# SwiGLU gate and up products: a pair's second block takes S2 before S1, blocks 1 to 10 begin S2's PSUM bank with the kept sum, and bank copies get a higher priority

## The chip, the cores and the metric

The kernel runs on one core of one Trainium2 chip. The metric is the device time of one execution in microseconds (us), lower is better. The core's engines each work through a queue of their own: PE (TensorE, matmuls, with PEld for its weight loads), DVE (VectorE), ACT (ScalarE), POOL (GpSimd, used here mostly to issue DMAs) and SP (SyncE, which issues DMAs). Matmuls write into PSUM, which has eight banks; a bank holds one 128 x 512 result in float32.

## The reference

One encoder block: a token mixer, then a SwiGLU feed-forward layer, each between two RMS norms. The change lies in the feed-forward layer's first product.

```
def swiglu(h, w_gate_up, w_down):
    gu = jnp.einsum("bsd,df->bsf", h, w_gate_up)
    g, u = jnp.split(gu, 2, axis=-1)
    return jnp.einsum("bsf,fd->bsd", jax.nn.silu(g) * u, w_down)
...
for l in range(DEPTH):
    h = rmsnorm(x, norm_mix_pre[l])
    m = mixer(h, w_in[l], b_f[l], conv_w[l], w_branch[l], w_out[l])
    x = x + rmsnorm(m, norm_mix_post[l])
    h = rmsnorm(x, norm_ffn_pre[l])
    f = swiglu(h, w_gate_up[l], w_down[l])
    x = x + rmsnorm(f, norm_ffn_post[l])
```

There are 1024 tokens, 1024 model columns and 2816 hidden columns, all in float32.

## The kernel before

**Products.** A float32 product is made from three matmuls on operands split into a high and a low part (`mm3`). ACT writes the high part (`hi`, a copy), DVE the low part (`lo`, source minus high). `prod` runs four blocks of 128 along the contraction, so a product on a 128 x 512 bank is 12 matmuls. Large products go by a Winograd form of Strassen's scheme: seven products A11, A12, A22, S1 to S4 of sums of weight blocks, each with its partner of the activations (B11, B21, B22, T1 to T4), whose results are summed to the four quarters.

**The gate and up product.** Hidden columns come in 22 blocks of 128 (`f` = 0 to 21); a block's gate and up weights and the two halves of the tokens are the four quarters. A block's weights are loaded by SP (`raw` tiles, 512 KB each), summed on DVE (`sx`, and in place in `raw`) and split. Three kinds of operand pairs come out of it: one for A11 and A12 (`prep_first`), one for S2 and S3 (from `sx`), one for S1 and A22 (from the second `raw`) (`prep_rest`). Their tiles come from one pool: three `raw`, four `hi`, three `lo`, one `sx`. A tile can be written again when the last product that reads it is done.

**Blocks 0 to 10** had A11 and A12 done in an earlier stage (`f_begin`, `f_end`). Two sums of each are kept: `p1` (A11's product) and `g1` (the gate quarter). For blocks 0 and 1 they stay in the tile `um`, for the others they go through DRAM (`pre_dram`) and come back by loads that POOL issues, into two tiles for `p1` and two for `g1`. Class `Rest` (from line 2098) does what is left: S2 into bank `b2`; DVE adds `p1` to it, giving `c12`; ACT copies `c12` back into the bank; S1 goes into `b3`; S3 is accumulated on `b2`; ACT copies the bank to `c22`, DVE adds `b3`; A22 is accumulated on `b2`, S4 on `b3`; ACT takes the Silu of `g1` and DVE multiplies it with `b2`. The loop at line 2129 interleaves two blocks, so that PE's order is S3(f), S2(f+1), A22(f), S4(f), S1(f+1), S3(f+1).

**Block 11** goes alone (`strassen`). **Blocks 12 to 21** go in five pairs x, y (`two_blocks`, line 2052): each has six products of its own, and their S4 products are done together by a second level of the scheme, seven half-width products (`prod2`, six matmuls of 256 columns each) into bank `zb` and the halves of `b3`. The loop fixes PE's order:

```
for step in (x.a11, x.s1, x.s2, x.a12, x.s3):
    step()
more()
for step in (y.a11, x.a22, y.s1, y.s2, y.a12, y.s3):
    step()
```

after which come the half-width products, with y.a22 before the last of them. `more()` prepares the next pair's x block (`prep_even`). In a block, A11, S2, S3 and A22 are accumulated one upon the other in bank `b1`, and after each ACT copies the bank out (`c11`, `c12`, `c22`) before the next is added; the tiles for these are halves of `um`.

**Order on the engines.** PE's order in the pair stage is the program's (`strict`). The order on ACT, DVE, POOL and SP is made when the kernel is built, by a planner that gives each engine, among the instructions that it holds to be ready, the one with the best priority; priority is the place in the program, and `ahead(call, by)` (line 125) moves it `by` places to the front. On the chip each engine then works in that fixed order.

**Afterwards** come the down product (bank names `pd`) and the last norm, with PE busy to the end.

Of the kernel before, what the change touches and what calls it, by code (L numbers as in the profile page):

```python
# [36 lines left out]
VF = AW + H  # L37
HV = VF // 2
TAIL = 4
NPRE = 11  # L40


B11, B21, B22, T1, T2, T3, T4 = range(7)
A11, A12, A22, S2, S3, S4, S1 = range(7)
# [3 lines left out]
def block_kernel(  # L48
# [16 lines left out]
    n1, n2 = slice(0, NC), slice(NC, S)  # L65
# [44 lines left out]
    def add(o, a, b):  # L110
        nc.vector.tensor_tensor(o, a, b, op=ALU.add)
# [13 lines left out]
    def ahead(call, by=80):  # L125
        with tc.high_priority(offset=by):
            call()

    def copy(o, a):
        nc.scalar.activation(o, a, AF.Copy)  # L130

    def split(hi, lo, src):

        copy(hi, src)
        sub(lo, src, f32(hi))

    def mm3(ps, a, b, start, stop, **kw):

        ah, al = a
        bh, bl = b  # L140
        nc.tensor.matmul(ps, ah, bh, start=start, stop=False, **kw)
        nc.tensor.matmul(ps, ah, bl, start=False, stop=False, **kw)
        nc.tensor.matmul(ps, al, bh, start=False, stop=stop, **kw)
# [14 lines left out]
    }  # L158
    pre_dram = [dpool.tile([2, P, NC], F32, name=f"pre_dram{f}") for f in range(NPRE)]
    ri_dram = [dpool.tile([2, S], F32, name=f"ri_dram{j}") for j in range(4)]  # L160
# [383 lines left out]
    def raw_t():  # L544
        return wtile("raw", 3)

    def hi_t():
        return wtile("hi", 4, F32R)

    def lo_t():  # L550
        return wtile("lo", 3, F32R)
# [10 lines left out]
    def kmaj(src):  # L562
        return src.rearrange("(k p) m -> p k m", p=P)
# [3 lines left out]
    def prep_first(src1, there=None):  # L567

        if there is None:
            r1 = raw_t()  # L570
            nc.sync.dma_start(r1, kmaj(src1))
            h1, l1 = hi_t(), lo_t()
            split(h1, l1, r1)
        else:
            r1, h1, l1 = there
        return dict(A11=(h1[:, LO], l1[:, LO]), A12=(h1[:, UP], l1[:, UP])), r1

    def prep_rest(src2, r1, behind=False, keep=None):

        r2 = raw_t()  # L580
        nc.sync.dma_start(r2, kmaj(src2))
        a11, a12, a21, a22 = r1[:, LO], r1[:, UP], r2[:, LO], r2[:, UP]
        sx = wtile("sx", 1)
        s2, s3 = sx[:, LO], sx[:, UP]
        (pinned if behind else lambda call, _: call())(lambda: sub(s3, a11, a21), "vector")
        s1 = a21
        add(s1, a21, a22)
        sub(s2, s1, a11)
        hx, lx = hi_t(), lo_t()
        split(hx, lx, sx)  # L590
        h2, l2 = hi_t(), lo_t()
        split(h2, l2, r2)
        ops = dict(
            S2=(hx[:, LO], lx[:, LO]), S3=(hx[:, UP], lx[:, UP]),
            S1=(h2[:, LO], l2[:, LO]), A22=(h2[:, UP], l2[:, UP]),
        )
        s4 = a12 if keep == "there" else s4_t()
        sub(s4, a12, s2)
        if keep:
            return {**ops, "S4": s4, "raw": r1}  # L600
        h4, l4 = s4h_t(), s4l_t()
        split(h4, l4, s4)
        return {**ops, "S4": (h4, l4)}
# [13 lines left out]
    def prod(ps, w, b, first):  # L617
        (ah, al), (bh, bl) = w, b
        kw = {} if first else dict(skip_group_check=True)
        for k in range(4):  # L620
            mm3(
                ps,
                (ah[:, k, :], al[:, k, :]),
                (bh[:, k, :], bl[:, k, :]),
                first and k == 0,
                k == 3,
                **kw,
            )
# [63 lines left out]
    def wcols(c0):  # L692
        return win[:, c0 : c0 + P]
# [352 lines left out]
    for ij, (kind, j, _, _) in enumerate(jobs):  # L1046
# [12 lines left out]
        if ij < 2:  # L1059
            if ij == 0:  # L1060
                r1 = raw_t()
# [13 lines left out]
            w = {**w, **prep_rest(wcols(jobs[ij][3]), r1)}  # L1075
# [3 lines left out]
        elif ij < len(jobs) - 1:  # L1079
# [3 lines left out]
            w = pairs.get()  # L1083
# [3 lines left out]
        else:  # L1087
            w = pairs.get()
# [14 lines left out]
        elif kind == "gb":  # L1103
            for m, parts in ((j, (c11, c12)), (j + 1, (c21, c22))):
                zt = zts.pop(m)
                for n in range(2):
                    o = n * NC
# [340 lines left out]
    def both(t):  # L1448
        return t[:, 0], t[:, 1]
# [320 lines left out]

    FIRSTS = [*range(2, NPRE), 0, 1]
    begun, kept = {}, {}
# [21 lines left out]
    hb = [both(h2b11)]  # L1794
# [84 lines left out]

    for n in range(4, NPRE + 1):  # L1880
        if n < NPRE:
            f_begin(n, bank(psm, "b1"), first_tile(n, "c21", 7))
# [4 lines left out]
        if n == 8:  # L1887
            for sl in range(4):
                a = slice(sl * P, (sl + 1) * P)
                b = slice(NC + sl * P, NC + (sl + 1) * P)  # L1890
# [29 lines left out]
    def gated(f, ns, g, u, t=None):  # L1920
        y = y_slot(f)[:, ns]
        t = y if t is None else t
        nc.scalar.activation(t, g, AF.Silu)
        mul(y, t, u)
# [14 lines left out]
    left, right = slice(0, NC // 2), slice(NC // 2, NC)  # L1939
# [62 lines left out]

    def prep_even(f):
        a, b = f_src(f)
        w, r1 = prep_first(a)
        return {**w, **prep_rest(b, r1, keep="own")}

    def prep_odd(f, even):
# [5 lines left out]
    class Block:  # L2014
# [5 lines left out]
        def a11(self):  # L2020
            self.b1, self.c11 = bank(psm, "b1"), t_(later, "c21")
            prod(self.b1, self.w["A11"], hb[B11], True)
            copy(self.c11, self.b1)

        def s1(self):
            self.b3 = bank(psm, "b3")
# [2 lines left out]
        def s2(self):  # L2029
            self.c12 = t_(later, "c12")  # L2030
            prod(self.b1, self.w["S2"], hb[T2], False)
            copy(self.c12, self.b1)

        def a12(self):
            b2 = bank(psm, "b2")
            prod(b2, self.w["A12"], hb[B21], True)
            add(self.c11, self.c11, b2)

        def s3(self):
            self.c22 = t_(later, "c22")  # L2040
            prod(self.b1, self.w["S3"], hb[T3], False)
            copy(self.c22, self.b1)
            add(self.c22, self.c22, self.b3)

        def a22(self):
            prod(self.b1, self.w["A22"], hb[T4], False)
            gated(self.f, n1, self.c11, self.b1)

        def end(self):
            gated(self.f, n2, self.c12, self.c22)  # L2050
# [1 line left out]
    def two_blocks(x, y, w2, more):  # L2052

        tq = um[:, 7, n1]
        for step in (x.a11, x.s1, x.s2, x.a12, x.s3):
            step()
        more()
        for step in (y.a11, x.a22, y.s1, y.s2, y.a12, y.s3):
            step()
        zb_ = bank(psm, "zb")  # L2060
        prod2(zb_[:, right], w2["S1"], hb2[T1], True)
        prod2(zb_[:, left], w2["A11"], hb2[B11])
        copy(tq[:, left], zb_[:, left])
        prod2(x.b3[:, left], w2["A12"], hb2[B21])
        prod2(x.b3[:, right], w2["S4"], hb2[B22])
        add(x.c12, x.c12, x.b3)
        prod2(y.b3[:, left], w2["A22"], hb2[T4])
        add(y.c12, y.c12, y.b3)
        prod2(zb_[:, left], w2["S2"], hb2[T2])
        copy(tq[:, right], zb_[:, left])  # L2070
        y.a22()
        prod2(zb_[:, left], w2["S3"], hb2[T3])

        def ends():
            add(x.c12, x.c12, tq)
            for b in (x, y):
                add(b.c12[:, right], b.c12[:, right], zb_[:, right])
            for n in (left, right):
                add(y.c12[:, n], y.c12[:, n], zb_[:, left])
            x.end()  # L2080
            y.end()

        return ends
# [9 lines left out]

    rest = Pairs([f_src(f) for f in range(NPRE)], prep_rest_alone)
    for _ in range(2):
        rest.more()

    class Rest:


        def __init__(self, f):
            self.f, self.w = f, rest.get(False)
            if f in kept:
                self.p1, self.g1 = kept[f]
            else:
                self.p1 = t_(fp, "c21")
                nc.gpsimd.dma_start(self.p1, pre_dram[f][0])
                self.g1 = z_tile("c11", w=NC)
                nc.gpsimd.dma_start(self.g1, pre_dram[f][1])
            self.b2, self.c12 = bank(psm, "b2"), t_(fp, "c12")  # L2110
            prod(self.b2, self.w["S2"], hb[T2], True)
            add(self.c12, self.p1, self.b2)
            copy(self.b2, self.c12)

        def two(self):
            self.b3, self.c22 = bank(psm, "b3"), t_(fp, "c22")
            prod(self.b3, self.w["S1"], hb[T1], True)
            prod(self.b2, self.w["S3"], hb[T3], False)
            copy(self.c22, self.b2)
            add(self.c22, self.c22, self.b3)  # L2120

        def end(self):
            prod(self.b2, self.w["A22"], hb[T4], False)
            prod(self.b3, self.w["S4"], hb[B22], False)
            gated(self.f, n1, self.g1, self.b2, self.g1)
            add(self.c12, self.c12, self.b3)
            gated(self.f, n2, self.c12, self.c22, self.c12)

    now = Rest(0)
    for f in range(NPRE):  # L2130
        now.two()
# [17 lines left out]
    for f in range(NPRE + 1, NF, 2):  # L2149
# [4 lines left out]
        x, y = Block(f, even), Block(f + 1, odd)  # L2154
# [275 lines left out]
```

## Time and profile before

| what | value |
|---|---|
| median of 3 runs | 1320.42 us (1319.51 to 1320.93) |
| the profiled execution's own time | 1319.99 us |
| its span in the trace | 1318.2 us |
| mean granted TensorE clock | 0.998 of full speed |
| stage of blocks 0 to 11, in the trace | about 737 to 907 us |
| five pairs, in the trace | about 907 to 1101 us |
| down product and the end | 1101 us to the end |

The profile shows one execution: busy time by engine, the waits with what ended them, the chain of work that ended last, and the instructions in order of time. A name such as `lo<-raw,hi` is "output <- inputs" by tile names; `b` stands for the banks `b1`, `b2` and `b3`, `c` for tiles such as `c12`, `c22`, `c21`. All instructions show line 77, the helper that issues them, so the tile names tell them apart. A matmul's row spans 0.39 us, but the next one starts about 0.227 us after it.

### The profile page before, as it was taken

The numbers are of one execution on the slowest core, as the hardware profiler recorded it, in microseconds if no ns is written. First come the engines' busy times: TensorE is split into PE (matmuls) and PEld (weight loads), VectorE is DVE, ScalarE is ACT, GpSimd is POOL, SyncE is SP. The second block draws the span as 40 slices with busy tenths as digits, with TensorE's granted clock in tenths as the row PEclk, the third lists the DMA queues.
The fourth block names the chain that finished last, engine by engine and source line by source line (L and its number), as shares of the span: only waits on it lengthen the run. The fifth ranks groups of instructions, "written<-read, shape, count | busy, mean of one in ns | idle before, by whom it ended". The sixth has DMA issues, their size and how long they took to land.

```text
span 1318.2 us, 18276 instructions
## 1 busy us (share of the span) xinstructions
PE 1302.3 (99%) x6776; PEld 1087.7 (83%) x6776; DVE 966.5 (73%) x1509; ACT 608.4 (46%) x977; POOL 154.9 (12%) x289
## 2 busy tenths in 40 slices
PE   9999999999999999999999999999999999999997
PEld 9988888888888888888878888888888788888886
DVE  6975979875656877587797677777676667676685
ACT  6642433253355866445677434333343334444452
POOL 0001100011112212020012012211100110000000
PEclk9999999999999999999999999999999999999999
DMA  6347757768646544499376456543322338866441
GB/s 219 112 119 224 196 161 208 191 211 232 176 144 200 162 140 157 148 346 367 114 242 207 134 162 194 188 130 102 120 78 99 104 120 292 304 249 195 157 167 65
DMA packets 207242, 235.15 MB, mean 178 GB/s; under 512 B 12064, under 2 KB 150368, under 8 KB 207152
## 3 DMA queue, kind: packets, MB, share of 16 engines
q1 hardware_dynamic: 159136, 156.08, 37.7%
q0 software_dynamic: 18832, 63.22, 13.1%
q10 hardware_dynamic: 29184, 14.68, 4.5%
q8 instruction: 53, 0.87, 0.3%
q14 instruction: 37, 0.30, 0.1%
HBM read 161.79 MB, written 72.16 MB: 177 GB/s over the span
## 4 chain that ended last, share of the span: by engine, by line
PE 91%; DVE 3%; ACT 2%; DMA 2%; issue 1%; DVEq 0%; POOL 0%; ACTq 0%; POOLq 0%
PE b L77 52%; PE pd L77 16%; PE pba L77 3%; PE pv L77 3%; PE tps L77 3%; PE po L77 3%; PE sp L77 2%; PE p L77 2%; PE pbp L77 2%; PE pbv L77 1%; PE zb L77 1%; DMA raw<-in_w_gate_up_dram 1%; DVE lo L77 1%; PE ma L77 1%; PE q L77 1%
## 5 line engine op out<-in xcount | busy, mean ns | idle before, releaser
L77 PE MATMUL b<-x,hi 128*128 128x512 f32 x1088 | 335.8, 390 | 0.7 <-ACT b L77 0.7
L77 PEld LDWEIGHTS b<-x,hi 128*128 128x128 f32 x1088 | 203.4, 188 | 43.1 <-ACT b L77 1.1
L77 PE MATMUL b<-x,lo 128*128 128x512 f32 x544 | 212.6, 391 | 4.3 <-DVE lo L77 4.3
L77 DVE TENSOR_TENSOR lo<-raw,hi 128x1024 fp32r<-128x1024 f32 x90 | 108.4, 1204 | 89.7 <-PE b L77 71.0
L77 ACT ACTIVATE hi<-raw 128x1024 fp32r<-128x1024 f32 (+1 forms) x96 | 97.4, 1017 | 80.5 <-PE b L77 43.0
L77 PEld LDWEIGHTS b<-x,lo 128*128 128x128 f32 x544 | 102.1, 188 | 27.8 <-DVE lo L77 6.8
L77 DVE TENSOR_TENSOR c<-c,b 128x512 f32<-128x512 f32 x120 | 81.7, 682 | 30.8 <-PE b L77 22.6
L77 ACT ACTIVATE hi<-sx 128x1024 fp32r<-128x1024 f32 (+1 forms) x42 | 43.8, 1042 | 80.9 <-PE b L77 71.6
L77 DVE TENSOR_TENSOR sx<-raw 128x512 f32<-128x512 f32 x78 | 53.6, 688 | 24.4 <-DMA raw<-in_w_gate_up_dram 12.6
L77 DVE TENSOR_TENSOR lo<-sx,hi 128x1024 fp32r<-128x1024 f32 (+1 forms) x42 | 50.3, 1197 | 27.4 <-PE b L77 24.3
L77 PE MATMUL pd<-hi,lo 128*128 128x512 f32 x160 | 62.3, 389 | 0.0
L77 PE MATMUL pd<-hi 128*128 128x512 f32 x160 | 61.9, 390 | 0.0
L77 PE MATMUL pd<-ghi 128*128 128x512 f32 x148 | 57.6, 389 | 0.0
L77 PE MATMUL pd<-ghi,glo 128*128 128x512 f32 x148 | 57.6, 389 | 0.0
L77 PE MATMUL pd<-glo,ghi 128*128 128x512 f32 x148 | 57.6, 389 | 0.0
L77 PE MATMUL b<-hT34h,lo 128*128 128x512 f32 x136 | 52.9, 389 | 0.0
L77 PE MATMUL b<-hT12h,hi 128*128 128x512 f32 x136 | 52.9, 389 | 0.0
L77 PE MATMUL b<-hT12l,hi 128*128 128x512 f32 x136 | 52.9, 389 | 0.0
L77 PE MATMUL b<-hT34h,hi 128*128 128x512 f32 x136 | 52.9, 389 | 0.0
L77 PE MATMUL b<-hT34l,hi 128*128 128x512 f32 x136 | 52.9, 389 | 0.0
L77 PE MATMUL b<-hT12h,lo 128*128 128x512 f32 x136 | 52.9, 389 | 0.0
L77 ACT ACTIVATE pt<-pt,nm 128x1024 f32<-128x1024 f32 (+7 forms) x62 | 47.0, 760 | 8.8 <-DVE nm L77 8.5
(504 smaller groups left out, 3123.1 us busy)
## 6 DMA issues: line engine op xcount, KB each, us to landing
raw<-in_w_gate_up_dram SPq DMA_DIRECT2D x55, 512.0 KB, 3.9
raw<-in_w_in_dram SPq DMA_DIRECT2D x35, 512.0 KB, 4.5
x<-wo_dram SPq DMA_DIRECT2D x28, 512.0 KB, 7.1
a_dramS<-um POOLq DMA_DIRECT2D x44, 256.0 KB, 2.5
a_dramA<-um POOLq DMA_DIRECT2D x33, 256.0 KB, 3.5
wo_dram<-h ACTq DMA_DIRECT2D x16, 448.0 KB, 4.3
wo_dram<-l ACTq DMA_DIRECT2D x16, 448.0 KB, 6.9
sg<-sg_dram SPq DMA_DIRECT2D x28, 256.0 KB, 3.0
```

The lines of the kernel that those rows point to most:

```text
L77: ins = getattr(self.engine, name)(*args, **kw)
```

## The change

Three edits. In a pair, y's S2 product now comes before its S1 product. In blocks 1 to 10, ACT copies `p1` into bank `b2` before S2, which is then accumulated on it; `c12` is a copy of the bank by ACT, in place of a DVE add and an ACT copy back. Block 0 has no copy into the bank: `c12`, `c22` and the last sum each get `p1` by a DVE add. And the copies and sums that read a bank, as well as `prep_first` in `prep_even` (load, high and low split of the next x block's first weights), are put 400 places ahead in the planner's priority.

```
-NPRE = 11
+NPRE, OUT = 11, 400
...
     def prep_even(f):
         a, b = f_src(f)
-        w, r1 = prep_first(a)
+        got = []
+        ahead(lambda: got.extend(prep_first(a)), OUT)
+        w, r1 = got
         return {**w, **prep_rest(b, r1, keep="own")}
...
             prod(self.b1, self.w["A11"], hb[B11], True)
-            copy(self.c11, self.b1)
+            ahead(lambda: copy(self.c11, self.b1), OUT)
...
             prod(self.b1, self.w["S2"], hb[T2], False)
-            copy(self.c12, self.b1)
+            ahead(lambda: copy(self.c12, self.b1), OUT)
...
-            add(self.c11, self.c11, b2)
+            ahead(lambda: add(self.c11, self.c11, b2), OUT)
...
-            copy(self.c22, self.b1)
-            add(self.c22, self.c22, self.b3)
+
+            def out():
+                copy(self.c22, self.b1)
+                add(self.c22, self.c22, self.b3)
+
+            ahead(out, OUT)
...
             prod(self.b1, self.w["A22"], hb[T4], False)
-            gated(self.f, n1, self.c11, self.b1)
+            ahead(lambda: gated(self.f, n1, self.c11, self.b1), OUT)
...
-        for step in (y.a11, x.a22, y.s1, y.s2, y.a12, y.s3):
+        for step in (y.a11, x.a22, y.s2, y.s1, y.a12, y.s3):
             step()
...
             self.b2, self.c12 = bank(psm, "b2"), t_(fp, "c12")
-            prod(self.b2, self.w["S2"], hb[T2], True)
-            add(self.c12, self.p1, self.b2)
-            copy(self.b2, self.c12)
+            if f:
+                ahead(lambda: copy(self.b2, self.p1), OUT)
+            prod(self.b2, self.w["S2"], hb[T2], not f)
+            ahead(lambda: self.take(self.c12, self.b2), OUT)
+
+        def take(self, o, b):
+            copy(o, b) if self.f else add(o, self.p1, b)
...
-            copy(self.c22, self.b2)
-            add(self.c22, self.c22, self.b3)
+
+            def out():
+                self.take(self.c22, self.b2)
+                add(self.c22, self.c22, self.b3)
+
+            ahead(out, OUT)
...
-            gated(self.f, n1, self.g1, self.b2, self.g1)
-            add(self.c12, self.c12, self.b3)
+
+
+            def out():
+                if not self.f:
+                    add(self.p1, self.p1, self.b2)
+                gated(self.f, n1, self.g1, self.b2 if self.f else self.p1, self.g1)
+                add(self.c12, self.c12, self.b3)
+
+            ahead(out, OUT)
             gated(self.f, n2, self.c12, self.c22, self.c12)
```

In `two_blocks`, the copies of `zb` to `tq` and the adds of `b3` to `c12` are wrapped in `ahead` in the same way.

More of the change, by code (lines that the diff above doesn't have):

```diff
@@ L2062, in two_blocks @@
         prod2(zb_[:, left], w2["A11"], hb2[B11])
-        copy(tq[:, left], zb_[:, left])
+        ahead(lambda: copy(tq[:, left], zb_[:, left]), OUT)
         prod2(x.b3[:, left], w2["A12"], hb2[B21])
         prod2(x.b3[:, right], w2["S4"], hb2[B22])
-        add(x.c12, x.c12, x.b3)
+        ahead(lambda: add(x.c12, x.c12, x.b3), OUT)
         prod2(y.b3[:, left], w2["A22"], hb2[T4])
-        add(y.c12, y.c12, y.b3)
+        ahead(lambda: add(y.c12, y.c12, y.b3), OUT)
         prod2(zb_[:, left], w2["S2"], hb2[T2])
-        copy(tq[:, right], zb_[:, left])
+        ahead(lambda: copy(tq[:, right], zb_[:, left]), OUT)
         y.a22()
```

## The prediction

> **What bounds the kernel now.** I read the busy shares first, then PE's waits, then the chain that ended last, and only then the queues around the places that these named. First the shares, then PE's waits on `b` banks (in us: total, how often, longest):
>
> ```profile
> PE 1302.3 (99%) x6776; PEld 1087.7 (83%) x6776; DVE 966.5 (73%) x1509; ACT 608.4 (46%) x977; POOL 154.9 (12%) x289
> PE b L77 <- DVE lo L77: 4.3, 5, 0.9
> PE b L77 <- ACT b L77: 0.7, 1, 0.7
> ```
>
> PE is the bound nearly throughout, so an edit that removes no matmul can gain only what PE waits. The change removes none: what it can win in its two stages is these six waits and the few slow matmuls behind them. The chain gives them places (start and length in us):
>
> ```profile
> 743.26 182.74 PE b L77 x804
> 926.02 1.24 DVE lo L77
> 927.30 10.73 PE b L77 x46
> 945.80 19.08 PE b L77 x84
> 964.91 1.23 DVE lo L77
> 1003.81 1.24 DVE lo L77
> 1042.73 1.23 DVE lo L77
> 1081.65 1.24 DVE lo L77
> 1101.42 209.77 PE pd L77 x924
> ```
>
> The five waits for `lo` come once in each pair. From 743.26 to 926.0, blocks 0 to 11 and the first pair's beginning, and again in the down product, PE runs without a break. 84 matmuls in 19.08 us make a pitch of 0.227 us, so a product of 12 takes 2.73 us.
>
> **The swap of y.S1 and y.S2.** PE around the first of the five waits, and DVE at the same place (start, length, instruction, and in brackets the idle time before it and what ended that):
>
> ```profile
> 925.82 0.61 PE L77 MATMUL b<-x,hi 128*128 128x512 f32 x2
> 927.30 0.50 PE L77 MATMUL b<-x,lo 128*128 128x512 f32 x1 [0.87 <-DVE lo L77]
> 937.87 0.28 PE L77 MATMUL zb<-hch,s4h 128*128 128x256 f32 x1
> ...
> 917.93 1.23 DVE L77 TENSOR_TENSOR lo<-raw,hi 128x1024 fp32r<-128x1024 f32 x1 [5.69 <-PE b L77]
> 920.73 1.22 DVE L77 TENSOR_TENSOR lo<-sx,hi 128x1024 fp32r<-128x1024 f32 x1
> 925.47 0.42 DVE L77 TENSOR_TENSOR l2b<-raw,l2b 128x256 fp32r<-128x256 f32 x1
> 926.02 1.23 DVE L77 TENSOR_TENSOR lo<-raw,hi 128x1024 fp32r<-128x1024 f32 x1
> 927.16 0.68 DVE L77 TENSOR_TENSOR um<-um,b 128x512 f32<-128x512 f32 x1
> ```
>
> Four products (48 matmuls: y.S1, y.S2, y.A12, y.S3) end where the first `zb` matmul starts, at 937.87. They began at 925.82 and should take 48 x 0.227 = 10.90 us; they took 12.05. So the wait costs 1.15 us with its slow restart, 5.75 us over five pairs.
>
> Why it waits: there are three `lo` tiles and six are needed per pair, so y's three take over x's three in turn. x's third, for S1 and A22, is read last by x.A22, the product directly before y.S1; only at its end, at about 926.0, can DVE write y's, and y.S1's third matmul needs it. In the new order y.S2 stands between. Its `lo` is the one from `sx`, done at 920.73 + 1.22 = 921.95, and its first use is at 925.82 + 2 x 0.227 = 926.27: 4.3 us of room. y.S1's `lo` still starts at 926.02 and is done at 927.25, and is now wanted at 926.27 + 2.73 = 929.00: 1.75 us of room where 0.98 were missing. DVE may put that much other work before it: the sum that now follows it (0.68, `um<-um,b` at 927.16) and one more of that length.
>
> What else moves with the two products: no DMA, and 12 matmuls past 12. S2 is accumulated on the bank that y.A11 filled, so ACT's copy of that bank must be done before y.S2:
>
> ```profile
> 923.30 0.60 ACT L77 ACTIVATE um<-b 128x512 f32<-128x512 f32 x1 [0.35 <-PE b L77]
> ...
> 742.61 0.60 ACT L77 ACTIVATE b<-c 128x512 f32<-128x512 f32 x1 [0.83 <-DVE c L77]
> 853.62 0.63 ACT L77 ACTIVATE c<-c 128x512 f32<-128x512 f32 x1 [2.52 <-DMA c<-pre_dram]
> 855.13 0.60 ACT L77 ACTIVATE c<-b 128x512 f32<-128x512 f32 x1 [0.88 <-PE b L77]
> ```
>
> It is done at 923.90, x.A22 lies between, and 1.9 us remain. The copy of y.S2's result, before y.S3, gets two products of time instead of one. I count nothing for these, and 5.75 us gained. If ACT's copy slipped by over 1.9 us, PE would pay the excess.
>
> The tile comes free no earlier than before, but it is wanted one product later. [...]
>
> **Block 0's bank.** PE and DVE before S3 of block 0:
>
> ```profile
> 742.18 0.39 PE L77 MATMUL b<-x,lo 128*128 128x512 f32 x1
> 743.26 0.73 PE L77 MATMUL b<-x,hi 128*128 128x512 f32 x2 [0.69 <-ACT b L77]
> ...
> 739.34 1.23 DVE L77 TENSOR_TENSOR lo<-sx,hi 128x1024 fp32r<-128x1024 f32 x1 [0.41 <-ACT hi L77]
> 741.28 0.69 DVE L77 TENSOR_TENSOR s4l<-s,s4h 128x512 fp32r<-128x512 f32 x1 [0.72 <-ACT s4h L77]
> 741.89 0.68 DVE L77 TENSOR_TENSOR c<-um,b 128x512 f32<-128x512 f32 x1
> ```
>
> S3 could start at 742.18 + 0.227 = 742.41 and starts at 743.26, 0.85 us late. The chain is S2's result, DVE's add (done 742.57), ACT's copy back (742.61, 0.60). The copy back goes, so even with the add in its old place S3 starts at about 742.6: 0.64 gained. S2 ended one product before 742.41, at 739.7, and DVE's add stood behind a split that waited for ACT; with 400 places of priority it can follow the split that ends at 740.57, and all 0.85 goes. I take 0.85. The add of `p1` to `c22` and to the last sum (two DVE instructions of 0.68) has A22's and S4's time, or is wanted by no product.
>
> **Blocks 1 to 10.** Per block ACT's copy back and DVE's add go; a copy of `p1` into the bank and a copy out of it come. These are the groups of 743 to 880 us (count, total us, mean ns), and the stage's busy times:
>
> ```profile
> 743.00:880.00 137.00, 136.74 (x603) 113.22 (x604) 100.97 (x140) 48.94 (x68) 24.95 (x46) 1.00 0.52 163
> L77 ACT ACTIVATE b<-c 128x512 f32<-128x512 f32 x11 | 6.6, 602 | 32.3 <-DVE c L77 32.3
> L77 ACT ACTIVATE c<-b 128x512 f32<-128x512 f32 x10 | 6.0, 599 | 22.3 <-PE b L77 22.3
> c<-pre_dram POOLq DMA_DIRECT2D x18, 256.0 KB, 3.5
> 764.09 0.54 POOL L77 DMA_DIRECT2D c<-pre_dram  x1 [5.85 <-DVE c L77]
> ```
>
> ACT gains 10 x 0.60 = 6.0 us on 48.9 of 137 busy; DVE loses 10 x 0.68. PE gains nothing, as it did not wait here. What is new is that PE waits for ACT before S2. The seed needs `p1` and a free bank. S2 of block f starts 2.73 + (f - 1) x 13.64 us after 743.26 (five products per block), so block 4's starts at 786.9. Its `p1` was issued at 764.09 (the first load that waits for a tile, when block 2's sum has let it go) and takes 3.5 us: it lands at 767.6, 19 us early, and the tile that it waits for now comes free earlier still, when the seed is copied and not when S2 is added. Of eight banks a block uses two, so a bank is free too. The longest hold-up on ACT is a Silu waiting for `g1`, worst 2.52 us: it ends at 854.25, with S2 of block 9 due at 855.1. Even a seed behind it is done at 854.85. So I take 0; the least is also 0, the most is in the rivals.
>
> **Priority.** It adds no instruction. SP's loads, ACT's high and DVE's low split of the next x block cannot run before a tile is free; in the row below DVE idled 2.71 us until PE let go the tile for that split, so an earlier place brings nothing, and sums of 0.68 put before splits have the rooms given above.
>
> ```profile
> 935.42 1.23 DVE L77 TENSOR_TENSOR lo<-raw,hi 128x1024 fp32r<-128x1024 f32 x1 [2.71 <-PE b L77]
> ```
>
> **Sum.** 5.75 + 0.85 = 6.6 us. The profiled execution took 1319.99 us (its span is 1318.2, in which the stages behind keep their length, as PE has no break there): 1313.4. The median lies 0.43 above that execution, so I forecast 1313.8 for the median.
>
> **The rivals.**
>
> *The wait shrinks or moves within the pair* (0.16). The planner's times are not the chip's, and the sums with priority may stand before y.S1's `lo` while still waiting for PE. With three or four such (0.61 apart, as 741.28 and 741.89) the room of 1.75 us is used up and 0.1 to 0.7 us stay per pair, 0.5 to 3.5 in all; likewise a seed a few tenths late in some blocks. Result 1314.3 to 1317.3, still faster. For it: DVE is 73% busy. Against it: DVE idled 5.69 and 2.71 us in front of two of these splits.
>
> *The gap stays, or comes back elsewhere* (0.12). If y.S1's `lo` came later by as much as it is wanted later, because tiles are short either way, the five waits stay and only block 0's 0.85 is won: 1319.6. [...] Or `prep_first`, 400 places early (four to five blocks of some 85 instructions), takes a `lo` tile out of turn: the last blocks run on two tiles, with a split of 1.22 us between S3 and the next S2, 1.4 with restart, four or five times, 6 us, which eats the gain: 1319.8. Against it: y.S1's `lo` hangs on x.A22's end, which does not move, and x and y need all three tiles in turn.
>
> *Slower: the seed behind the wrong copy* (0.08). If ACT gets the seed of block f+1 behind the copy of block f's `c22`, PE stops in every block: S3 ends at the moment when S2 should start; that copy starts about 0.3 us later (855.13 in the row), ends at 855.73, the seed 0.60 after, with slow restart about 1.5 us in all, ten times: 15 us, 1328.8. It decides once the seed starts less than 0.6 us before S2. For it: ACT waited seven times, 12.6 us in all, for a `g1` load just before these copies, and a seed queued there waits too:
>
> ```profile
> ACT c L77 <- DMA c<-pre_dram: 12.6, 7, 2.5
> ```
>
> Against it: the 19 us by which `p1` is early. [...]
>
> That the priorities change no order is no rival of its own: the swap and the seeds are fixed by the program, and the result would be 1313.8 + 0.2.
>
> **How the numbers follow.** The forecast has 0.64, the first rival 0.16; both are faster by over 0.2% (2.6 us), about what a measurement can tell from no change: 0.80. The second rival gives same, 0.12; the third slower, 0.08. The range of 0.8 is that of the first two: below, 1312.5, which is the forecast less the 0.9 us by which the lowest of the runs shown lies under their median, and 0.4 of slow restarts that I may have missed; above, 1317.6, the first rival's end with a little of the same spread.
>
> **What would show it.** Right: no PE wait for `lo` in the pairs; a pair's period down from 38.9 (964.91 to 1003.81) to 37.75 us; S3 of block 0 without a wait; no wait of PE for ACT before S2; the `pd` matmuls beginning at about 1094.8. The swap's step is wrong if PE still waits for `lo` once a pair, the seed's if the waits name ACT `b` ten times.

## The result and the profile after

The changed kernel takes 1313.67 us (median of 5 runs, 1313.23 to 1314.2) against 1320.42 before (median of 5 runs, 1319.51 to 1320.93). The ratio is 0.9949, with a 95% interval of 0.9935 to 0.9964. The forecast was 1313.8 with a range of 1312.5 to 1317.6. The profiled execution took 1313.5 us with a span of 1311.7, so the two spans differ by 6.5 us.

The busy shares and PE's waits on `b` banks from block 0 to the down product, after the change (us in total, how often, longest):

```profile
PE 1300.5 (99%) x6776; PEld 1087.5 (83%) x6776; DVE 964.2 (74%) x1501; ACT 610.4 (47%) x985; POOL 154.9 (12%) x289
PE b L77 <- DVE c L77: 0.5, 1, 0.5
```

The five waits for `lo` are gone, and nothing has come in their place but one wait in block 0. The chain that ended last, after the change (start, length, what, number of matmuls):

```profile
742.86 193.51 PE b L77 x852
936.37 1.43 PE zb L77 x12
...
944.14 29.95 PE b L77 x132
974.09 1.43 PE zb L77 x12
...
1087.25 1.43 PE zb L77 x12
...
1095.02 209.73 PE pd L77 x924
```

Before, the chain left PE for a `lo` split in every pair (46 matmuls, a split, 84 matmuls). Now it stays on PE from S3 of block 0 to the down product. The step from one `zb` to the next is the pair's period, 37.72 us against 38.9. From S3 of block 0 to the first `pd` matmul it was 1101.42 - 743.26 = 358.16 us and is now 1095.02 - 742.86 = 352.16. Of these 6.0 us, 5.9 are five pairs at 1.18 each. Block 0's S3 starts 0.40 us earlier, and the down product to the end of the span is 0.1 shorter: 6.5 in all.

VectorE and TensorE around the first pair's y.S2 and y.S1, after the change (start, length, instruction, and in brackets the idle time before it with what ended it):

```profile
925.53 0.69 DVE L77 TENSOR_TENSOR um<-um,b 128x512 f32<-128x512 f32 x1 [0.28 <-PE b L77]
926.13 1.22 DVE L77 TENSOR_TENSOR lo<-raw,hi 128x1024 fp32r<-128x1024 f32 x1
```

```profile
925.33 0.61 PE L77 MATMUL b<-x,hi 128*128 128x512 f32 x2
...
928.05 0.61 PE L77 MATMUL b<-x,hi 128*128 128x512 f32 x2
928.50 0.39 PE L77 MATMUL b<-x,lo 128*128 128x512 f32 x1
```

y.S2 runs from 925.33 to 928.05. y.S1's `lo` is done at 927.35 and is wanted at 928.50, the third matmul of y.S1: 1.15 us are left. The sum `um<-um,b`, which followed the split before, now stands ahead of it, as the prediction allowed for one or two such sums.

Blocks 1 to 10, after the change: the engines in 743 to 880 us (length, then busy us and counts of PE, PEld, DVE, ACT and POOL, granted clock, DMA share, GB/s), two of ScalarE's groups there (count, total us, mean ns, idle time before them), and one seed (ACT's copy of `p1` into the bank) with a later copy of `c22`:

```profile
743.00:880.00 137.00, 137.00 (x605) 113.43 (x606) 97.70 (x132) 52.95 (x75) 25.25 (x47) 1.00 0.52 163
```

```profile
L77 ACT ACTIVATE c<-b 128x512 f32<-128x512 f32 x19 | 11.4, 599 | 47.3 <-PE b L77 47.3
...
L77 ACT ACTIVATE b<-c 128x512 f32<-128x512 f32 x9 | 5.2, 582 | 0.0
```

```profile
795.18 0.58 ACT L77 ACTIVATE b<-c 128x512 f32<-128x512 f32 x1
...
800.31 0.60 ACT L77 ACTIVATE c<-b 128x512 f32<-128x512 f32 x1 [2.81 <-PE b L77]
```

PE is busy for all 137.00 us. The seed `b<-c` is done at 795.76, and the copy of `c22` starts only at 800.31, when S3 of that block has ended and the seeded S2 begins: the seed is over four us early.

### The profile page after: what moved, and what is told of

Read it like the earlier page. It is cut to its first block, busy times and chain, and to the rows that moved or that the text cites. A ratio compares the mean times of both kernels' runs of the same rounds, so it can differ in the third digit from the quotient of the medians.

```text
span 1311.7 us, 18264 instructions
## 1 busy us (share of the span) xinstructions
PE 1300.5 (99%) x6776; PEld 1087.5 (83%) x6776; DVE 964.2 (74%) x1501; ACT 610.4 (47%) x985; POOL 154.9 (12%) x289
## 4 chain that ended last, share of the span: by engine, by line
PE 92%; DVE 3%; DMA 2%; ACT 2%; issue 1%; SPq 0%; DVEq 0%; POOL 0%; ACTq 0%
PE b L77 54%; PE pd L77 16%; PE pba L77 3%; PE pv L77 3%; PE po L77 2%; PE tps L77 2%; PE p L77 2%; PE sp L77 2%; PE pbp L77 2%; PE pbv L77 1%; PE zb L77 1%; PE ma L77 1%; PE q L77 1%; PE tp L77 1%; DMA raw<-in_w_gate_up_dram 1%
## 5 line engine op out<-in xcount | busy, mean ns | idle before, releaser
L77 DVE TENSOR_TENSOR c<-c,b 128x512 f32<-128x512 f32 x111 | 75.7, 682 | 28.8 <-PE b L77 22.4
L77 DVE TENSOR_TENSOR um<-um,b 128x512 f32<-128x512 f32 x47 | 31.9, 685 | 36.6 <-PE b L77 36.0
L77 ACT ACTIVATE c<-b 128x512 f32<-128x512 f32 x49 | 28.8, 593 | 59.7 <-PE b L77 56.2
```

The lines of the kernel that those rows point to most:

```text
L77: ins = getattr(self.engine, name)(*args, **kw)
```

## The experiments

Each is compared with runs of the kernel before on the same chip. The edits are shown against the kernel named.

### Which of the three edits pays: swap_only, seeds_only, no_swap, no_priority

`swap_only` is the kernel before with the new order alone:

```
-        for step in (y.a11, x.a22, y.s1, y.s2, y.a12, y.s3):
+        for step in (y.a11, x.a22, y.s2, y.s1, y.a12, y.s3):
```

> The kernel before with one edit: y.S2 before y.S1. Theory (the gaps come from y.S1's low split, which waits for x.A22 to let its tile go, and the swap alone hides it): the five PE waits for lo are gone, a pair takes 37.7 us in place of 38.9, block 0's wait of 0.7 us stays; 5 x 1.19 = 6.0 us less than before, 1314.5 us. Rival (the priorities or the lighter DVE work of blocks 1 to 10 closed the gaps): the waits stay, 1320 us.

Measured: 1314.62 us (1313.36 to 1317.24), ratio 0.9962 (0.9949 to 0.9974). The chain in its trace:

```profile
936.14 1.43 PE zb L77 x12
...
973.86 1.43 PE zb L77 x12
...
1094.79 209.73 PE pd L77 x924
```

No wait for `lo`, period 37.72, and `pd` begins at 1094.79, where the whole change has 1095.02. From S3 of block 0 on that is 352.26 us (742.53 to 1094.79) beside 352.16: in this stretch the swap alone gives what the whole change gives.

`seeds_only` is the changed kernel with the old order and without the 400 places:

```
     def ahead(call, by=80):
+        if by == OUT:
+            return call()
```

> The changed kernel with neither the swap nor the priorities: the seeds alone. Theory: the five waits for lo are as before (0.9 us), only block 0's chain is 0.64 us shorter: 1319.1 us against 1319.7 of the kernel before on this chip, no difference to be measured. Rival (the longer gaps of the run without the swap came from the seeds, not from the priorities): gaps of 1.5 us and 1322.7 us.

Measured: 1319.29 us (1317.69 to 1321.79), ratio 0.9998 (0.9989 to 1.0007): no difference. Its waits are those of the kernel before:

```profile
PE b L77 <- DVE lo L77: 4.3, 5, 0.9
```

`no_swap` is the changed kernel with the old order, priority and seeds kept.

> The changed kernel with y.S1 before y.S2 again, seeds and priorities kept. Theory: the five waits are back, and longer, because the sum that the priority now puts ahead of y.S1's low split (0.61 us from start to start) delays it: 1.2 + 0.6 us a pair against none, 1313.7 + 9 = 1322.7 us, slower than before. If that sum costs nothing: 1319.7 us. Rival (priorities or seeds closed the gaps): 1314 us.

Measured: 1323.29 us (1321.83 to 1323.88), ratio 1.0025 (1.0016 to 1.0034). VectorE, then TensorE in the second pair:

```profile
966.33 0.69 DVE L77 TENSOR_TENSOR um<-um,b 128x512 f32<-128x512 f32 x1 [0.34 <-PE b L77]
966.94 1.22 DVE L77 TENSOR_TENSOR lo<-raw,hi 128x1024 fp32r<-128x1024 f32 x1
```

```profile
968.21 0.50 PE L77 MATMUL b<-x,lo 128*128 128x512 f32 x1 [1.47 <-DVE lo L77]
```

The priority puts the sum of 0.61 us ahead of the split. In the old order there is no room for it, and the wait grows from 0.87 to 1.47. In the new order the same move costs nothing. So the priority does harm without the swap, and none here with it.

`no_priority` is the changed kernel with the edit of `ahead` shown above and the new order.

> The changed kernel without the 400 places of priority (swap and seeds kept). Theory (the priorities bring nothing): 1313.7 us within 0.5, no wait for lo in the pairs, no wait for the seeds. Rival (the priorities are needed so that seeds or splits come in time): waits of PE for ACT before S2, or for lo, of 0.3 us or more each, 1316 to 1325 us.

Measured: 1313.31 us (1311.58 to 1313.9), ratio 0.995 (0.9937 to 0.9962). No wait for `lo` and none for a seed; the pair's period is 37.72 again. The 400 places bring nothing that a median shows. In block 0 they cost something, which comes out below.

### Is it the tile, or the order: own_lo

The claim was that y.S1 waits because three `lo` tiles are too few for the old order. Then another tile must do the same as the swap. Not a whole fourth `lo` tile, but one of 1 KB per partition for the first two of y.S1's four blocks along the contraction, was added to the kernel before, with the old order:

```
+            early = t2.tile([P, 2, P], F32R, tag="e2", name="early", bufs=1)
+            copy(h2, r2)
+            sub(early, r2[:, e2], f32(h2[:, e2]))
+            sub(l2[:, u2], r2[:, u2], f32(h2[:, u2]))
```

> The kernel before, no swap, with 1 KB per partition of further room: the low part of y.S1's first two blocks has a tile of its own, so that only the last two wait for x.A22. Theory (a tile that is not free makes the gap): the late part is wanted 8 matmuls (1.8 us) after y.S1's begin and is done about 1.2 us after it, so the waits are gone without any swap, 1314.5 us. If the gap has another cause, such as DVE being late with its queue: the waits stay, 1320 us.

Measured: 1314.69 us (1312.82 to 1316.39), ratio 0.9961 (0.9948 to 0.9973), beside 0.9962 for the swap. VectorE around y.S1, and the chain:

```profile
924.12 0.42 DVE L77 TENSOR_TENSOR early<-raw,hi 128x256 fp32r<-128x256 f32 x1
...
928.38 0.95 DVE L77 TENSOR_TENSOR lo<-raw,hi 128x768 fp32r<-128x768 f32 x1
```

```profile
976.83 1.43 PE zb L77 x12
...
1014.55 1.43 PE zb L77 x12
```

The small tile is written at 924.12, before x.A22 ends, and the rest of the low part follows when x's tile is free. The period is 37.72 here too. More memory and a later use are two cures of one shortage, worth the same.

### How much room the swap left: lo_twice, lo_thrice

In the changed kernel, y's low split for S1 and A22 is done twice, or three times, into the same tile. No work is left out.

```
         split(h2, l2, r2)
+        for _ in range(1 if keep == "there" else 0):
+            sub(l2, r2, f32(h2))
```

> The changed kernel, with the low split of y's second weights (y.S1 and y.A22) done twice over, so that it ends 1.14 us later, 5 pairs. Theory (after the swap the split has 1.10 us to spare: done at 927.35, wanted at 928.50, and 0.05 for the signal): the room is just used up, waits of at most 0.1 us a pair, 1313.7 to 1314.4 us. Rival (the swap leaves no room, or DVE's load matters as a whole): about 1.1 us a pair, 1319 us.

Measured: 1315.52 us (1315.4 to 1315.86), ratio 0.9966 (0.9952 to 0.9979). VectorE and TensorE in its second pair:

```profile
964.42 2.48 DVE L77 TENSOR_TENSOR lo<-raw,hi 128x1024 fp32r<-128x1024 f32 x2
```

```profile
966.33 0.61 PE L77 MATMUL b<-x,hi 128*128 128x512 f32 x2
966.95 0.50 PE L77 MATMUL b<-x,lo 128*128 128x512 f32 x1
```

The two splits end at 966.90. The `lo` matmul was due at 966.33 + 0.45 = 966.78 and starts at 966.95. The period is 38.06 (936.94 to 975.00), 0.34 more than 37.72. The start is late by 0.17, and the other 0.17 is a slow pitch behind it. The profile lists no wait for so short a gap. So the 1.15 us of room are real: 1.26 us of further work (2.48 less 1.22) goes just past them. The time is 1.1 us above the expected range, which had at most 0.1 a pair: it counted 1.14 for the second split and nothing for the slow pitch.

> The same with the split done three times, 2.28 us later, as it would be if other work stood before it. Theory: 1.2 us over the room, with slow restart 1.3 us a pair, 1313.7 + 6.5 = 1320.2 us. Rival (something else than this split releases y.S1): no wait, 1313.7 us.

Measured: 1329.02 us (1327.22 to 1330.21), ratio 1.0066 (1.0051 to 1.0082): a miss by nearly 9 us. VectorE, then TensorE in its second pair, then the engines in its second and third period (columns as above):

```profile
966.52 2.48 DVE L77 TENSOR_TENSOR lo<-raw,hi 128x1024 fp32r<-128x1024 f32 x2
969.39 0.69 DVE L77 TENSOR_TENSOR sx<-raw 128x512 f32<-128x512 f32 x1 [0.39 <-DMA raw<-in_w_gate_up_dram]
970.00 1.22 DVE L77 TENSOR_TENSOR lo<-raw,hi 128x1024 fp32r<-128x1024 f32 x1
```

```profile
971.27 0.50 PE L77 MATMUL b<-x,lo 128*128 128x512 f32 x1 [2.22 <-DVE lo L77]
971.61 0.99 PE L77 MATMUL b<-x,hi 128*128 128x512 f32 x2
972.40 0.63 PE L77 MATMUL b<-x,lo 128*128 128x512 f32 x1
```

```profile
939.04:980.89 41.85, 39.63 (x189) 33.14 (x188) 29.61 (x43) 14.77 (x23) 3.80 (x7) 0.96 0.28 94
980.89:1021.42 40.53, 38.01 (x188) 31.98 (x188) 29.59 (x43) 14.77 (x23) 3.81 (x7) 1.00 0.30 98
```

Two things were not in the expectation. The planner put a sum for the next block between the second and the third split, and that sum waited for its load, so the wait is 2.22 us where a third split alone would have made some 1.3 (the fifth pair has no such sum and waits 1.26). And in the second period the granted clock is 0.96, and PE's busy time is 1.6 us longer than in the third (39.63 against 38.01): behind the wait the matmuls come 0.4 us apart, not 0.227, until 975.26. The fourth period is like the second. The waits add up to 10.3 us of the 15.25 by which `pd` starts later than in the changed kernel (1110.27 against 1095.02), the lowered clock in two periods to some 3.2, and the rest is about the slow restart seen in the third period (38.01 of PE's busy time against 37.72, 0.3 a pair, 1.5 over five) and 0.25 by which block 0's S3 is later in this run. The experiment answers its question: once the room is gone, the wait is there in every pair.

### The slower rival: seed_late, seed_strict

In the changed kernel the seed of a block is pinned behind the `c22` copy of the block before on ScalarE, from block 2 on (block 1's stays early). `sow` does what `Rest` did at its beginning, and in lines not shown the copy and the seed are held to the program's order on ScalarE:

```
         now.two()
         rest.more()
+        if f + 1 < NPRE:
+            sown[f + 1] = sow(f + 1)
```

> The changed kernel, with ACT's copy of p1 into the bank kept behind the copy of the block before's c22, for blocks 2 to 10. Theory (PE waits for the seed; the price of the slower rival): each of nine blocks waits from the end of S3 for the c22 copy (0.33 + 0.5 us) and the seed (0.60), 1.45 us, 1.6 with restart: 1313.7 + 14.4 = 1328.1 us. Rival (a late seed is hidden or takes less): 1313.7 to 1320 us.

Measured: 1322.04 us (1320.5 to 1323.38), ratio 1.0013 (1.0004 to 1.0022): 8.4 us over the changed kernel's median, where the rival had 15. ScalarE, then TensorE, at one block:

```profile
789.41 0.60 ACT L77 ACTIVATE c<-b 128x512 f32<-128x512 f32 x1 [2.52 <-PE b L77]
789.90 0.60 ACT L77 ACTIVATE b<-c 128x512 f32<-128x512 f32 x1
```

```profile
789.21 0.39 PE L77 MATMUL b<-x,hi 128*128 128x512 f32 x1
790.06 1.23 PE L77 MATMUL b<-x,hi 128*128 128x512 f32 x4 [0.46 <-ACT c L77]
```

PE goes on at 790.06, before the seed is done at 790.50, so what runs there cannot be S2. Three other matmuls stand ahead of S2: one of the next S1 (789.21) and two of A22, which need only the copy (790.06 and one pitch later). The loop does not fix PE's order, and the planner filled the hole. 3 x 0.227 = 0.68 us of the wait are covered, and a block is 0.79 longer (14.39 against 13.60). `seed_strict` takes that away by fixing PE's order in the loop:

```
     now = Rest(0)
+    strict[0] = ("tensor",)
     for f in range(NPRE):
```

> As seed_late (the seeds of blocks 1 to 10 stand behind the copy of c22 on ScalarE), but with TensorE's order of the changed kernel kept through the loop over blocks. In seed_late the planner put three other matmuls (one of the next S1, two of A22) ahead of S2, 3 x 0.227 = 0.68 us of the wait. Theory: the price of the slower rival was right and was hidden by this. Then a block is longer by 0.79 + 0.68 = 1.47 us, or by 1.3 if only the two copies count (S3's last matmul ends 789.37, the copy and the seed behind it end 790.50, S2 could have begun at 789.21): 1326.7 to 1328.4 us, with ten waits of TensorE for ScalarE's seed of about 0.9 to 1.2 us each and no matmul between S3 and S2. Rival: the two copies cost only 0.8 us a block in any order of TensorE: 1322.0 us again.

Measured: 1328.34 us (1327.32 to 1329.19), ratio 1.006 (1.0047 to 1.0074). ScalarE and TensorE at the same block, and TensorE's waits:

```profile
788.67 0.60 ACT L77 ACTIVATE c<-b 128x512 f32<-128x512 f32 x1 [2.76 <-PE b L77]
789.16 0.60 ACT L77 ACTIVATE b<-c 128x512 f32<-128x512 f32 x1
```

```profile
788.24 0.39 PE L77 MATMUL b<-x,lo 128*128 128x512 f32 x1
789.81 0.73 PE L77 MATMUL b<-x,hi 128*128 128x512 f32 x2 [1.18 <-ACT b L77]
```

```profile
PE b L77 <- ACT b L77: 11.3, 9, 1.9
```

Now S2 waits for the seed in nine blocks. In eight of them the wait is 1.18 us and a block takes 15.08 us (774.73 to 789.81) against 13.60, 1.48 more: the rival's 1.5. In the ninth the seed is later still, by a split queued ahead of it: the wait is 1.90, and TensorE goes on slowly:

```profile
881.00 0.91 PE L77 MATMUL b<-x,hi 128*128 128x512 f32 x2 [1.90 <-ACT b L77]
881.71 0.63 PE L77 MATMUL b<-x,lo 128*128 128x512 f32 x1
```

That makes up for the tenth block, which the rival had counted and which has no late seed: `pd` begins at 1109.67, and at 1094.64 in the changed kernel run beside it (`after_again`), 15.0 us; counted from S3 of block 0, 367.80 against 352.19, it is 15.6. So the rival's price for a block was right, its count one too many; and it needs that nothing else can be put before S2.

### Block 0: seed0, seed0_plain, after_again

`seed0` seeds block 0 too, `seed0_plain` is that without the 400 places, `after_again` is the changed kernel once more. In the first two the sum put into block 0's bank counts in the last 128 of its 512 columns only (worked out from the output in the last section), so these are no versions to use; the instructions are those of a full one.

```
-            if f:
-                ahead(lambda: copy(self.b2, self.p1), OUT)
-            prod(self.b2, self.w["S2"], hb[T2], not f)
+            ahead(lambda: copy(self.b2, self.p1), OUT)
+            prod(self.b2, self.w["S2"], hb[T2], False)
```

> The changed kernel with block 0 seeded as well, so that VectorE's two adds and TensorE's wait for VectorE's c in block 0 fall away. Theory (block 0's 0.5 us wait is for the add that stands behind the late load, Silu and split): the stretch from the sx row to S3 of block 0 shrinks from 8.10 to about 7.4 us, no wait of TensorE for VectorE's c is left there, and the time is 0.5 to 0.8 us under the changed kernel: 1312.9 to 1313.2 us, which the medians can hardly tell from 1313.67. Rival (the load alone holds TensorE there, the adds cost nothing): 8.1 us again and 1313.7 us. A third way: the seed waits for a load of c21 itself and the wait moves to the first S2: no gain or a loss of up to 0.6 us.

> As seed0, without the 400 places of priority. Theory (the priority put the Silu ahead of the split and cost 0.5 us in block 0, and there is no add left to be hurried): the sx row to S3 of block 0 is 7.0 to 7.6 us, 1312.7 to 1313.2 us. Rival (the priority was needed for the copies that empty the banks): waits of TensorE for ScalarE's copies appear in blocks 1 to 10, 0.2 us or more each, 1315 us or more.

> The changed kernel itself once more, as the measure for seed0 and seed0_plain on the same chip: 1313.2 to 1314.2 us by its five runs so far. In block 0 the stretch from the sx row to S3 is 8.1 us again, whatever the time at which the load lands; TensorE's recorded wait there may be anything from 0 to 2 us, as it has been between the other runs.

Measured: `seed0` 1312.07 us (1311.62 to 1313.88), ratio 0.994 (0.9928 to 0.9953); `seed0_plain` 1313.69 (1311.88 to 1315.97), 0.9952 (0.9938 to 0.9965); `after_again` 1313.18 (1312.79 to 1314.82), 0.9949 (0.9937 to 0.9962). The intervals overlap, and the medians say nothing here. The traces do: neither seeded kernel has a wait of PE in block 0, and `after_again` has it, for VectorE's `c`, 0.6 us.

```profile
741.10 0.73 PE L77 MATMUL b<-x,hi 128*128 128x512 f32 x2
```

In `seed0`, S3 of block 0 starts at 741.10, 7.26 us after the `sx` row that waits for the weight load; in `after_again` it is 8.10 (734.35 to 742.45), as in the first run of the changed kernel. The wait does hang on the add behind the late load. `seed0_plain` has no wait for ScalarE either, so the 400 places are not needed for the copies. Its stretch is a miss all the same: 8.25 us (733.37 to 741.62) where 7.0 to 7.6 were expected. The copy that S3 needs was done after 7.20 (740.57), but TensorE, busy without a gap, came to S3 only at 741.62: in that run the load was early, and TensorE's own work set the time.

## Why the prediction was right, and where it was not

**The swap, 5.75 us: right in cause and size.** The pairs gave 1.18 each (38.90 to 37.72), 6.0 from S3 of block 0 to the down product. `swap_only` shows that the swap does it alone, `own_lo` that the shortage of `lo` tiles was the cause, and `lo_twice` that the room was what the rows had said: 1.75 less the sum of 0.61 that came ahead of the split leaves 1.14, and 1.15 was read.

**Block 0's bank, 0.85 us: this term was mis-sized.** The path to S3 of block 0 begins at a weight load. From the `sx` row that the load releases to S3 it took 8.21 us before (735.05 to 743.26) and 8.10 after (734.76 to 742.86): 0.11 was won. The other 0.29 by which S3 starts earlier is the load landing earlier in that run. Counted from TensorE's last matmul before S3, as the prediction did, S3 is now 0.63 us late (742.00 + 0.227 to 742.86) where it was 0.85 and nothing was forecast. The step that failed was that the priority would put the add directly behind the split. ScalarE and VectorE there, after the change:

```profile
740.34 0.62 ACT L77 ACTIVATE um<-um 128x512 f32<-128x512 f32 x1
740.86 0.62 ACT L77 ACTIVATE s4h<-s 128x512 fp32r<-128x512 f32 x1
```

```profile
741.51 0.69 DVE L77 TENSOR_TENSOR s4l<-s,s4h 128x512 fp32r<-128x512 f32 x1 [1.24 <-ACT s4h L77]
742.12 0.68 DVE L77 TENSOR_TENSOR c<-um,b 128x512 f32<-128x512 f32 x1
```

The same two engines in `no_priority`:

```profile
740.48 0.62 ACT L77 ACTIVATE s4h<-s 128x512 fp32r<-128x512 f32 x1
741.00 0.62 ACT L77 ACTIVATE um<-um 128x512 f32<-128x512 f32 x1
```

```profile
741.13 0.69 DVE L77 TENSOR_TENSOR s4l<-s,s4h 128x512 fp32r<-128x512 f32 x1 [0.72 <-ACT s4h L77]
741.74 0.68 DVE L77 TENSOR_TENSOR c<-um,b 128x512 f32<-128x512 f32 x1
```

The add stayed behind `s4l` in both. The priority moved the Silu (`um<-um`), which is part of `gated`, ahead of `s4h`, for which `s4l` waits, and so made the add later by half a us. Without it the stretch is 7.57 us (734.90 to 742.47): 0.64 less than before, the floor that the prediction gave for an add left in its place. The price of the copy back was right, and the priority took most of it away again. That the totals agree, 6.6 forecast and 6.5 between the spans, is luck in this part: the pairs' stretch gave 0.25 more and the load landed early.

**The seeds, nothing: right.** PE has no wait for ScalarE in blocks 1 to 10, and ScalarE's work in 743 to 880 us rose from 48.94 to 52.95, VectorE's fell from 100.97 to 97.70. That is 4.0 more and 3.3 less where 6.0 and 6.8 were forecast; as neither engine holds PE up there, the sizes did not matter. `seeds_only` puts the seeds at 0.9998 (0.9989 to 1.0007).

**Priority, nothing: right by the medians,** but only in part for the reason given. The sum that it puts ahead of y's split is covered by the room that the swap made, as said. That it also moves block 0's Silu, which costs 0.53 (8.10 against 7.57), was not foreseen.

**The rivals.** The wait did not shrink or move within the pair: one sum came ahead of the split, where three would have been needed. The gap did not stay. `own_lo` shows that a tile that was not free was its cause (no wait for `lo`, period 37.72), and the swap that more memory is not the only cure. The seed behind the copy costs what was said per block (`seed_strict`), and it did not happen here since the seed is queued with four us to spare. In both late kernels the seed starts only behind the copy, at 789.90 and 789.16.

**The signs.** No wait for `lo`, the period (37.72 for 37.75), no wait for a seed and the start of `pd` (1095.02 for 1094.8) came as said. S3 of block 0 without a wait did not.

## What to carry to other kernels

A wait for a tile that repeats with the loop has two cures, another tile or a later use; if a neighbouring product has its operands early, moving it in between costs no memory and is priced as its length less what is missing. When an order is changed by priority, look at what else has the same priority on that engine: here it hurried a Silu past a high split on ScalarE, for which VectorE's instruction in front of the hurried add had to wait. And a wait forced into a kernel by way of experiment has to be looked at in the trace before its price is believed: a planner may fill it (`seed_late`) or lengthen it (`lo_thrice`).

## What the runs showed of the hardware

**Behind some waits of about two us the matmuls came more slowly.** After waits of 2.22 us (`lo_thrice`, shown above) and 2.18 in the same kernel, of 1.90 (`seed_strict`) and 1.92 (`own_lo`, block 0) the next matmuls came 0.4 us apart for 3.7 to 4.2 us. The granted clock was 0.57 there in `lo_thrice` (971.27 to 975.26), and in `seed_strict` 0.66 over 881 to 886, of which the slow matmuls are the greater part. After waits of 2.07 and 2.52 in `lo_thrice` the matmuls came 0.23 apart (clock 1.00 in 1013 to 1016, from just before the end of the longer wait). So in these runs the length of the wait does not decide it alone; what does was not tried.

**The landing of one load moved block 0 by more than this term is worth.** The `sx` row that it releases started between 733.77 (`seed_strict`) and 736.04 (`no_swap`), kernels with the same block 0 up to S3. In nine runs TensorE's last matmul before S3 starts 7.1 to 7.3 us after that row, so that most of this is a shift of the whole stream; but it is 7.8 in `swap_only` and 5.9 in `own_lo`, and accordingly, with the old block 0, PE's wait there was nothing in `swap_only` and 1.92 us in `own_lo`. A term of under one us behind such a load is read from the landing on, not from the span.

**In `seed0` the seed of block 0's PSUM bank was kept in one quarter only.** That `seed0` counts the sum in the last 128 columns only is worked out from the output: with the sum missing from the first three quarters of block 0's bank, the reference's formulas give a relative difference of 0.12776, and that of `seed0` and `seed0_plain` is 0.12776; with another quarter kept it would be 0.12873, 0.12782 or 0.12711. As block 0's loss alone gives this figure, the seeds of blocks 1 to 10 were kept whole. Why block 0's was not, and why the last quarter is the one that was, no run shows.
